# One operand of VectorE's two-input operations moved from SBUF to PSUM in the residual sums, the table scaling and the rotary embedding

## The chip, the core and the metric

One core of one Trainium2 chip runs the whole program; the other cores are idle. The metric is the device time of one execution in microseconds (us). The kernel before took 1189.33 us, the median of three runs that lie between 1189.12 and 1189.84 us.

The engines are named as in the profile: PE is TensorE's matmul, PEld its weight load, DVE is VectorE, ACT is ScalarE, POOL is GpSimd and SP is SyncE, which issues the weight DMAs. SBUF is the working memory. PSUM is the memory that matmuls write, here eight banks of 128 x 512 f32.

## The reference

The program computes two transformer blocks on 256 tokens of width 1024, in f32. Cut to what the change touches:

```
x = x + conv(norm(x));  x = x + mem_attention(norm(x), mem);  x = x + swiglu(norm(x))
k = rope(norm(x) @ w_k);  q = rope(norm(x) @ w_q)      # only 16 of 64 features of a head turn
x = x + diff_attention(q, k, v);  x = x + mem_attention(...);  x = x + swiglu(...)
x = norm(x, g_final);  h = norm(x, g_pre)              # first block ends, second begins
q, k_c, k_s, k_w, k_sw = rope(h @ w_in ...)            # 64 of 64 features turn, then sparse attention
x = x + norm(attention @ w_out);  x = x + norm(conv_swiglu(norm(x)))
rope: out1 = r1 * cos - r2 * sin,  out2 = r1 * sin + r2 * cos
```

## The kernel before

Activations are kept with features on the partitions: x is 8 chunks of 128 features by 256 tokens, and a pair of chunks fills one PSUM bank. Every projection is computed in three matmuls per weight tile, from a high part and a low part of weights and activations. A weight panel of 128 x 1024 is loaded by SP into one of six stage buffers. ACT then writes its high part `whi` (L276), and DVE or POOL subtracts to get the low part `wlo` (L278), from two operands in SBUF. Both go into a ring of five panels, so that the preparation runs five panels ahead of PE.

`gemm` (L392 on) runs over the panels and accumulates up to four banks (`acc`, six buffers). Its last `tail` panels are done bank by bank, so that the banks close one after another and `evac(b, ps)` of each is issued while PE works on the next. `resid` (L435 on) is the evacuation that ends a sublayer: it adds the bank to x, splits the new x times the next norm's gain into a high and a low part (`to_set`, L431 to L433, into S0 or S1), and adds its square to the norm's sum (`Stats.add`, ACT then POOL). It is used five times: after the convolution, both memory attentions, the first feed forward (with two targets, S0 and S1) and the differential attention. `last` (L947 on) does the same after the second feed forward, where two norms follow one another. The sum of squares is folded (`sfold`, L355), summed over the partitions by small matmuls (L361), raised to -1/2 on POOL, and spread over the partitions by a matmul with the identity into an `aux` bank (`spread`, L375 on), from which ACT copies it to SBUF as `Rb` (L381).

`tables` (L820) and `tables2` (L1000) multiply cosine and sine by that factor. `roped_k` and `roped` (L828 to L845) turn the keys and queries of the differential attention: a shuffle swaps the halves, two products follow and then the sum. The keys' sum is written in two halves of 64 partitions. `rope2` (L1008) does the same in the second block.

The differential attention runs a list of steps (`DIFF_SEQ`): q0 and q1 are projections of two heads' queries, a0, a1, ... the scores and softmax of a head (L867, L868 on PE, then `masked`, L324, on DVE), V0 and V1 the values, b the transposed weights, c the values' sum, f the norm of two heads (L908 to L923). PE runs them in the order written. The second block's attention has a like list (`ATT_SEQ`).

The tile framework places every semaphore. A planner with a cost model of its own orders each engine's queue, so that the order on DVE and ACT need not be the order of the program. Two engines that access one PSUM bank are made to take turns. A pool's tag with `bufs=2` gives two buffers in turn. The tag `sq` is that of the squares in `Stats` and of the window in the second block (L1070).

Of the kernel before, what the change touches and what calls it, by code (L numbers as in the profile page):

```python
# [21 lines left out]
F32 = mybir.dt.float32  # L22
# [14 lines left out]
# ---------------------------------------------------------------- layout of the inputs  # L37
# [23 lines left out]
# order of the steps of the two attention parts that share the tensor engine with their projections:  # L61
# a: scores and softmax of a head, b: weights transposed, c: values, f: norm of two heads; the rest are projections
# [8 lines left out]
def _constants():  # L71
    c = np.zeros((128, NCST), np.float32)

    def put(name, a):
        o, n = COFF[name]
        c[:, o:o + n] = a

    i = np.arange(128)
    put("ident", np.eye(128))
    low = np.where(i[None, :] <= i[:, None], 0.0, NEG)  # L80
    put("mask0D", np.concatenate([np.zeros((128, 128)), low], 1))
    put("pair", np.concatenate([np.eye(30), np.eye(30), np.zeros((68, 30))]))
    put("maskUD", np.concatenate([np.where(i[None, :] > i[:, None], 0.0, NEG), low], 1))
    blk = np.arange(32)
    mc = np.zeros((128, 2, 32))
    for t in range(2):
        ok = (blk[None, :] < 15) & (blk[None, :] * 16 + 31 <= (t * 128 + i)[:, None])
        mc[:, t] = np.where(ok, 0.0, NEG)
    put("maskC", mc.reshape(128, 64))
    put("rowv", np.stack([(i >= 31), np.ones(128)], 1))  # L90
    inv = (np.float32(500000.0) ** (-np.arange(0, 16, 2, dtype=np.float32) / np.float32(16))).astype(np.float32)
    f, sg = np.zeros((128, 1), np.float32), np.zeros((128, 1), np.float32)
    for p in range(128):
        d = p % 64
        if d < 16:
            f[p], sg[p] = inv[d % 8], (-1.0 if d < 8 else 1.0)
    put("freq", f)
    put("sgn", sg)
    inv2 = (np.float32(10000.0) ** (-np.arange(32, dtype=np.float32) / np.float32(32))).astype(np.float32)
    ang = np.arange(S, dtype=np.float32)[None, :] * inv2[:, None]  # L100
    d = np.array([PERM[p % 64] for p in range(128)])
    put("cos2", np.cos(ang.astype(np.float64))[d % 32])
    put("sin2", np.sin(ang.astype(np.float64))[d % 32] * np.where(d < 32, -1.0, 1.0)[:, None])
    return c


def _layout(I):
# [30 lines left out]
    def sub(w, nk, W):  # L138
        # panels of nk row blocks by W columns, a column group's panels together
        K, M = w.shape[0] // 128, w.shape[1]  # L140
        return w.reshape(K // nk, nk, 128, M // W, W).transpose(3, 0, 2, 1, 4).reshape(-1, nk * W)
# [40 lines left out]
# ---------------------------------------------------------------- the program  # L182
@with_exitstack
def program(ctx: ExitStack, tc: tile.TileContext, A, out):
# [20 lines left out]
    # ---- weight panels: loaded and split ahead of use  # L205
    panels = []
# [81 lines left out]
    # ---- constants  # L288
# [6 lines left out]
    def vc(name, i=0):  # L295
        o, _ = VOFF[name]
        return vecs[:, o + i:o + i + 1]
# [24 lines left out]
    # scores with their mask and times -1/8, and with their least value, the bias of the exponent  # L322
# [3 lines left out]
    # ---- pieces  # L326
# [48 lines left out]
    def spread(r):  # L375
        pb = aux()
        for t in range(2):
            PE.matmul(pb[:, t * 128:(t + 1) * 128], r[:, t:t + 1].to_broadcast([128, 128]), ident,
                      start=(t == 0), stop=True, skip_group_check=True)
        Rb = tmp.tile([128, S], F32, name="Rb", tag="Rb")  # L380
        SC.activation(Rb, pb[:, :S], AF.Copy)  # L381
        return Rb
# [52 lines left out]
    def resid(stats, targets, bias=None):  # L435
        def f(j, ps):
            xp = x[:, 2 * j:2 * j + 2]
            if bias:
                for i in range(2):
                    c = 2 * j + i  # L440
                    V.scalar_tensor_tensor(x[:, c], ps[:, i * S:(i + 1) * S], vc(bias, c), x[:, c],
                                           op0=OP.add, op1=OP.add)
            else:
                V.tensor_tensor(xp, b2(ps), xp, op=OP.add)
            for st, gname, g0 in targets:
                for c in (2 * j, 2 * j + 1):
                    stats.low = to_set(st, c, x[:, c], vc(gname, g0 + c))
            stats.add(xp)
        return f

    # ================================================================ conformer convolution
# [28 lines left out]
    # memory operands  # L480
# [92 lines left out]
    # keys and values in two parts  # L573
# [27 lines left out]
    # layer norm  # L601
# [53 lines left out]
    # ================================================================ memory attention  # L655
# [84 lines left out]
    # rotary angles of the first block, reduced to [-pi, pi]  # L740
# [29 lines left out]
    # ================================================================ gated feed forward  # L770
# [37 lines left out]
    # ================================================================ differential attention  # L808
    rot = [(i + 8 if i < 8 else i - 8) if i < 16 else i for i in range(32)]
    with ExitStack() as es:  # L810
# [9 lines left out]
        def tables():  # L820
            rb = spread(st.r)
            G.memset(k[0:64, :, 1], 0.0)
            G.memset(k[64:128, :, 0], 0.0)
            V.tensor_tensor(cR, cosT, rb, op=OP.mult)
            V.tensor_tensor(sR, sinT, rb, op=OP.mult)

        def roped(dst, g=0):
            def f(j, ps):  # L828
                d = dst[:, 2 * (g + j):2 * (g + j) + 2]
                t = P.tile([128, 2, S], F32, name="rt", bufs=2)  # L830
                V.stream_shuffle(t.rearrange("p a t -> p (a t)"), ps, rot)
                V.tensor_tensor(d, b2(ps), two(cR), op=OP.mult)
                V.tensor_tensor(t, t, two(sR), op=OP.mult)
                V.tensor_tensor(d, d, t, op=OP.add)
            return f

        def roped_k(j, ps):
            t = P.tile([128, 2, S], F32, name="rt", bufs=2)
            t2 = b2(o[:, j % 2, 0:2 * S])
            V.stream_shuffle(t.rearrange("p a t -> p (a t)"), ps, rot)  # L840
            V.tensor_tensor(t2, b2(ps), two(cR), op=OP.mult)
            V.tensor_tensor(t, t, two(sR), op=OP.mult)
            for c in range(2):
                pr = slice(64 * c, 64 * c + 64)
                V.tensor_tensor(k[pr, 2 * j:2 * j + 2, c], t2[pr], t[pr], op=OP.add)  # L845
# [13 lines left out]
        def a_(h):  # L859
            # per component: query tile 0 on keys 0, query tile 1 on keys 0 and 1  # L860
# [17 lines left out]
        def b_(h):  # L878
            # p0 - lam * (sum0 / sum1) * p1; the factor 1 / sum0 joins the norm of the head
# [64 lines left out]
    # ================================================================ second block  # L944
    sa, sb = Stats(), Stats()

    def last(j, ps):  # L947
        xp = x[:, 2 * j:2 * j + 2]
        V.tensor_tensor(xp, b2(ps), xp, op=OP.add)
        sa.add(xp)  # L950
        for c in (2 * j, 2 * j + 1):
            V.tensor_scalar(x[:, c], x[:, c], vc("g_final", c), None, op0=OP.mult)
            to_set(S0, c, x[:, c], vc("g_pre", c))
        sb.add(xp)
# [31 lines left out]
    def norms():  # L986
        # r1 of the first block's last norm, r2 of the norm that follows it
# [12 lines left out]
    def tables2():  # L1000
        RB[0] = spread(rr)
        V.tensor_tensor(cR, cs("cos2"), RB[0], op=OP.mult)
        V.tensor_tensor(sR, cs("sin2"), RB[0], op=OP.mult)
# [4 lines left out]
    def rope2(d, ps, n):  # L1008
        t = P.tile([128, 2, S], F32, name="rt", bufs=2)
        V.stream_shuffle(t.rearrange("p a t -> p (a t)")[:, :n * S], ps[:, :n * S], rot2)  # L1010
        tb = lambda a: a[:, None, :].to_broadcast([128, n, S])
        V.tensor_tensor(d, ps[:, :n * S].rearrange("p (a t) -> p a t", a=n), tb(cR), op=OP.mult)
        V.tensor_tensor(t[:, :n], t[:, :n], tb(sR), op=OP.mult)
        V.tensor_tensor(d, d, t[:, :n], op=OP.add)  # L1014

    # gates: sigmoid = 1 / (1 + exp(-z))
# [35 lines left out]
    # blocks of the compressed branch: both heads' windows with (token pair, feature) on partitions  # L1052
# [24 lines left out]
    # x2, tokens on partitions  # L1077
# [16 lines left out]
    # rows 0 to 29 of a product come from the high part of the windows, rows 30 to 59 from the low part  # L1094
# [50 lines left out]
    # ---- sliding window heads  # L1145
# [44 lines left out]
    # ---- heads with three branches: 4 diagonal blocks, 2 full ones, 2 of the compressed keys  # L1190
# [108 lines left out]
    # ---- output projection, post norm, residual: tokens on partitions  # L1299
    def rms(hs):  # L1300
        # hs: [128, 2] mean squares of the two halves of a row, each over the whole row
# [120 lines left out]
```

## Time and profile before

| | |
|---|---|
| three runs | 1189.12, 1189.33, 1189.84 us |
| profiled execution, first to last instruction (its span) | 1183.8 us; the profile gives no other time of it |
| what lies around the span, against the runs' median | 5.5 us |
| PE busy | 1121.6 us, 95% of the span |
| PEld, DVE, ACT, POOL busy | 1061.5, 829.4, 639.5, 427.3 us |
| TensorE's granted clock, mean | 0.978 of full speed |
| HBM traffic | 160 GB/s over the span |

PE's busy time is modelled from pipelined matmuls. A matmul of 256 columns is shown as some 280 ns long, while the next one starts earlier than that. What PE loses is therefore read from its waits and from the granted clock, not from its busy share. [...]

### The profile page before, as it was taken

How to read it: one execution, taken by the hardware profiler on the slowest of the kernel's cores; microseconds unless marked ns; L12 is line 12 of the kernel's file. 1: busy time of each engine (PE TensorE's matmuls, PEld its weight loads, DVE VectorE, ACT ScalarE, POOL GpSimd, SP SyncE). 2: the span in 40 equal slices, each digit the busy share in tenths (PEclk: the TensorE clock that was granted, in tenths of full speed). 3: DMA queues.
4: the chain of work that ended last, by engine and by line, in shares of the span. 5: the costliest groups of instructions: out<-in, count | busy, mean ns of one | idle time of the engine just before them, and what ended most of it. 6: DMA issues, size and time to landing. Idle time of an engine off the chain costs nothing. (4 is left out here: it accounts for less than half of the span.)

```text
span 1183.8 us, 21512 instructions
## 1 busy us (share of the span) xinstructions
PE 1121.6 (95%) x8418; PEld 1061.5 (90%) x8418; DVE 829.4 (70%) x1452; ACT 639.5 (54%) x1114; POOL 427.3 (36%) x278
## 2 busy tenths in 40 slices
PE   7999988999999999597899999999898998999997
PEld 7998878999999999497899999999887677999986
DVE  6899867585766458777775746654978747787844
ACT  6564474555545354374555444543585645675642
POOL 5999845230000016565344544000654210111300
PEclk9999988999999999898999999999999999999999
DMA  7565534345546545342243554563664114454661
GB/s 266 192 240 211 189 114 158 110 152 192 181 150 225 194 143 182 107 158 89 90 142 125 194 199 163 174 226 121 187 193 177 37 54 160 161 191 157 219 199 36
DMA packets 59798, 191.13 MB, mean 161 GB/s; under 512 B 6752, under 2 KB 10080, under 8 KB 59696
## 3 DMA queue, kind: packets, MB, share of 16 engines
q1 hardware_dynamic: 58288, 187.31, 46.6%
q0 software_dynamic: 688, 1.90, 0.6%
q8 instruction: 66, 1.08, 0.4%
q10 hardware_dynamic: 720, 0.53, 0.1%
q14 instruction: 36, 0.29, 0.1%
HBM read 188.15 MB, written 1.05 MB: 160 GB/s over the span
## 5 line engine op out<-in xcount | busy, mean ns | idle before, releaser
L276 ACT ACTIVATE whi<-wf 128x1024 fp32r<-128x1024 f32 (+3 forms) x382 | 370.5, 985 | 324.0 <-PE acc L407 267.4
L278 DVE TENSOR_TENSOR wlo<-wf,whi 128x1024 fp32r<-128x1024 f32 (+3 forms) x251 | 311.5, 1252 | 166.3 <-ACT whi L276 165.5
L278 POOL TENSOR_TENSOR wlo<-wf,whi 128x1024 fp32r<-128x1024 f32 (+1 forms) x131 | 288.6, 2223 | 175.8 <-ACT whi L276 173.7
L407 PE MATMUL acc<-s0h,whi 128*128 128x256 f32 x1192 | 340.0, 286 | 5.4 <-ACT whi L276 5.4
L407 PE MATMUL acc<-s0h,wlo 128*128 128x256 f32 x1192 | 337.8, 284 | 3.1 <-POOL wlo L278 3.1
L407 PE MATMUL acc<-s0l,whi 128*128 128x256 f32 x1192 | 338.1, 284 | 2.7 <-DVE s0l L433 2.7
L407 PEld LDWEIGHTS acc<-s0h,whi 128*128 128x128 f32 x1192 | 228.7, 192 | 6.3 <-ACT whi L276 5.4
L407 PEld LDWEIGHTS acc<-s0h,wlo 128*128 128x128 f32 x1192 | 228.1, 191 | 4.5 <-POOL wlo L278 4.2
L407 PEld LDWEIGHTS acc<-s0l,whi 128*128 128x128 f32 x1192 | 228.4, 192 | 3.4 <-DVE s0l L433 3.1
L407 PE MATMUL acc<-s1l,whi 128*128 128x256 f32 x736 | 206.9, 281 | 2.7 <-DVE s1l L433 2.7
L407 PE MATMUL acc<-s1h,whi 128*128 128x256 f32 x736 | 206.7, 282 | 0.7 <-ACT s1h L645 0.7
L407 PE MATMUL acc<-s1h,wlo 128*128 128x256 f32 x736 | 206.2, 280 | 0.4 <-POOL wlo L278 0.4
L407 PEld LDWEIGHTS acc<-s1l,whi 128*128 128x128 f32 x736 | 138.9, 189 | 3.6 <-DVE s1l L433 3.3
L407 PEld LDWEIGHTS acc<-s1h,whi 128*128 128x128 f32 x736 | 138.8, 189 | 1.5 <-ACT s1h L645 1.4
L407 PEld LDWEIGHTS acc<-s1h,wlo 128*128 128x128 f32 x736 | 138.6, 188 | 0.6 <-POOL wlo L278 0.6
L338 POOL TENSOR_TENSOR sacc<-sq,sacc 128x512 f32<-128x512 f32 x21 | 33.6, 1600 | 291.9 <-ACT sq L337 291.5
L407 PE MATMUL acc<-hh,wlo 128*128 128x256 f32 x352 | 99.6, 283 | 0.0
L407 PE MATMUL acc<-hl,whi 128*128 128x256 f32 x352 | 99.6, 283 | 0.0
L407 PE MATMUL acc<-hh,whi 128*128 128x256 f32 x352 | 99.6, 283 | 0.0
L539 DVE SCALAR_TENSOR_TENSOR aux<-u,vecs,aux 128x256 f32<-128x256 f32 x174 | 68.6, 477 | 1.3 <-ACT aux L537 1.3
L407 PEld LDWEIGHTS acc<-hh,whi 128*128 128x128 f32 x352 | 67.6, 192 | 0.0
L407 PEld LDWEIGHTS acc<-hh,wlo 128*128 128x128 f32 x352 | 67.6, 192 | 0.0
(373 smaller groups left out, 1746.9 us busy)
## 6 DMA issues: line engine op xcount, KB each, us to landing
wf<-in_gu SPq DMA_DIRECT2D x120, 512.0 KB, 4.0
wf<-in_w_down SPq DMA_DIRECT2D x66, 512.0 KB, 4.0
wf<-in_mem_w_k SPq DMA_DIRECT2D x16, 512.0 KB, 4.0
wf<-in_mem_w_v SPq DMA_DIRECT2D x16, 512.0 KB, 3.5
wf<-in_mem_w_q SPq DMA_DIRECT2D x16, 512.0 KB, 3.5
wf<-in_mem_w_o SPq DMA_DIRECT2D x16, 512.0 KB, 3.9
wf<-in_w_pw SPq DMA_DIRECT2D x24, 256.0 KB, 3.0
wf<-in_gv SPq DMA_DIRECT2D x24, 256.0 KB, 2.6
```

The costliest lines, as they stand in the source:

```text
L276: p["ih"] = SC.activation(p["hi"][:, :W], p["f"][:, :W], AF.Copy)
L278: p["il"] = eng.tensor_tensor(p["lo"][:, :W], p["f"][:, :W], p["hi"][:, :W].bitcast(F32), op=OP.subtract)
L338: self.ins = self.eng.tensor_tensor(self.acc, sq, self.acc, op=OP.add)
L407: PE.matmul(o, l, r, start=(ki == 0 and n == 0 and q == 0), stop=(ki == K - 1 and q == 2), skip_group_check=True)
L539: V.scalar_tensor_tensor(cv[:, c] if k == TAPS - 1 else ai, src, w, ai, op0=OP.mult, op1=OP.add)
```

## The change

The operations keep their number or nearly so, but in each sum and product on DVE one operand is read from PSUM, and some results are written back into the bank that they came from. In `resid` the sum stays in the bank, `to_set` and the square read it there, and a new ACT copy brings it to x. In `last` the two gains are multiplied once (`gfp`), the sum stays in the bank as well, and two ACT copies with the final gain replace the two DVE products. The scale of the tables is read from the `aux` bank. The rotary embedding first multiplies by the sine table (whose signs are turned over), then multiplies the bank in place by the cosine table, shuffles the sine product, and adds it to the bank.

```diff
-            f[p], sg[p] = inv[d % 8], (-1.0 if d < 8 else 1.0)
+            f[p], sg[p] = inv[d % 8], (1.0 if d < 8 else -1.0)
...
-    put("sin2", np.sin(ang.astype(np.float64))[d % 32] * np.where(d < 32, -1.0, 1.0)[:, None])
+    put("sin2", np.sin(ang.astype(np.float64))[d % 32] * np.where(d < 32, 1.0, -1.0)[:, None])
...
-    def spread(r):
+    def spread(r, raw=False):
...
+        if raw:
+            return pb[:, :S]
         Rb = tmp.tile([128, S], F32, name="Rb", tag="Rb")
         SC.activation(Rb, pb[:, :S], AF.Copy)
         return Rb
...
     def resid(stats, targets, bias=None):
         def f(j, ps):
             xp = x[:, 2 * j:2 * j + 2]
+            half = [ps[:, i * S:(i + 1) * S] for i in range(2)]
             if bias:
                 for i in range(2):
                     c = 2 * j + i
-                    V.scalar_tensor_tensor(x[:, c], ps[:, i * S:(i + 1) * S], vc(bias, c), x[:, c],
-                                           op0=OP.add, op1=OP.add)
+                    V.scalar_tensor_tensor(half[i], half[i], vc(bias, c), x[:, c], op0=OP.add, op1=OP.add)
             else:
-                V.tensor_tensor(xp, b2(ps), xp, op=OP.add)
+                V.tensor_tensor(b2(ps), b2(ps), xp, op=OP.add)
             for st, gname, g0 in targets:
-                for c in (2 * j, 2 * j + 1):
-                    stats.low = to_set(st, c, x[:, c], vc(gname, g0 + c))
-            stats.add(xp)
+                for i in range(2):
+                    c = 2 * j + i
+                    stats.low = to_set(st, c, half[i], vc(gname, g0 + c))
+            stats.add(b2(ps))
+            SC.activation(xp, b2(ps), AF.Copy)
         return f
...
         def tables():
-            rb = spread(st.r)
+            rb = spread(st.r, raw=True)
...
+        def turned(ps):
+            t = P.tile([128, 2, S], F32, name="rt", bufs=2)
+            z = tmp.tile([128, 2, S], F32, name="rz", tag="sq")
+            V.tensor_tensor(t, b2(ps), two(sR), op=OP.mult)
+            V.tensor_tensor(b2(ps), b2(ps), two(cR), op=OP.mult)
+            V.stream_shuffle(z.rearrange("p a t -> p (a t)"), t.rearrange("p a t -> p (a t)"), rot)
+            return b2(ps), z
+
         def roped(dst, g=0):
             def f(j, ps):
                 d = dst[:, 2 * (g + j):2 * (g + j) + 2]
-                t = P.tile([128, 2, S], F32, name="rt", bufs=2)
-                V.stream_shuffle(t.rearrange("p a t -> p (a t)"), ps, rot)
-                V.tensor_tensor(d, b2(ps), two(cR), op=OP.mult)
-                V.tensor_tensor(t, t, two(sR), op=OP.mult)
-                V.tensor_tensor(d, d, t, op=OP.add)
+                t, z = turned(ps)
+                V.tensor_tensor(d, z, t, op=OP.add)
             return f
 
         def roped_k(j, ps):
-            t = P.tile([128, 2, S], F32, name="rt", bufs=2)
-            t2 = b2(o[:, j % 2, 0:2 * S])
-            V.stream_shuffle(t.rearrange("p a t -> p (a t)"), ps, rot)
-            V.tensor_tensor(t2, b2(ps), two(cR), op=OP.mult)
-            V.tensor_tensor(t, t, two(sR), op=OP.mult)
+            t, z = turned(ps)
             for c in range(2):
                 pr = slice(64 * c, 64 * c + 64)
-                V.tensor_tensor(k[pr, 2 * j:2 * j + 2, c], t2[pr], t[pr], op=OP.add)
+                V.tensor_tensor(k[pr, 2 * j:2 * j + 2, c], t[pr], z[pr], op=OP.add)
...
+    gfp = const.tile([128, 8], F32, name="gfp")
+    V.tensor_tensor(gfp, vecs[:, VOFF["g_final"][0]:VOFF["g_final"][0] + 8], vecs[:, VOFF["g_pre"][0]:VOFF["g_pre"][0] + 8], op=OP.mult)
 
     def last(j, ps):
         xp = x[:, 2 * j:2 * j + 2]
-        V.tensor_tensor(xp, b2(ps), xp, op=OP.add)
-        sa.add(xp)
-        for c in (2 * j, 2 * j + 1):
-            V.tensor_scalar(x[:, c], x[:, c], vc("g_final", c), None, op0=OP.mult)
-            to_set(S0, c, x[:, c], vc("g_pre", c))
+        V.tensor_tensor(b2(ps), b2(ps), xp, op=OP.add)
+        for i in range(2):
+            c = 2 * j + i
+            to_set(S0, c, ps[:, i * S:(i + 1) * S], gfp[:, c:c + 1])
+        sa.add(b2(ps))
+        for i in range(2):
+            c = 2 * j + i
+            SC.activation(x[:, c], ps[:, i * S:(i + 1) * S], AF.Copy, scale=vc("g_final", c))
         sb.add(xp)
...
     def tables2():
-        RB[0] = spread(rr)
-        V.tensor_tensor(cR, cs("cos2"), RB[0], op=OP.mult)
-        V.tensor_tensor(sR, cs("sin2"), RB[0], op=OP.mult)
+        rb = spread(rr, raw=True)
+        V.tensor_tensor(cR, cs("cos2"), rb, op=OP.mult)
+        V.tensor_tensor(sR, cs("sin2"), rb, op=OP.mult)
+        RB[0] = tmp.tile([128, S], F32, name="Rb", tag="Rb")
+        SC.activation(RB[0], rb, AF.Copy)
...
     def rope2(d, ps, n):
         t = P.tile([128, 2, S], F32, name="rt", bufs=2)
-        V.stream_shuffle(t.rearrange("p a t -> p (a t)")[:, :n * S], ps[:, :n * S], rot2)
+        z = tmp.tile([128, 2, S], F32, name="rz", tag="sq")
+        flat = lambda a: a.rearrange("p a t -> p (a t)")[:, :n * S]
         tb = lambda a: a[:, None, :].to_broadcast([128, n, S])
-        V.tensor_tensor(d, ps[:, :n * S].rearrange("p (a t) -> p a t", a=n), tb(cR), op=OP.mult)
-        V.tensor_tensor(t[:, :n], t[:, :n], tb(sR), op=OP.mult)
-        V.tensor_tensor(d, d, t[:, :n], op=OP.add)
+        pn = ps[:, :n * S].rearrange("p (a t) -> p a t", a=n)
+        V.tensor_tensor(t[:, :n], pn, tb(sR), op=OP.mult)
+        V.tensor_tensor(pn, pn, tb(cR), op=OP.mult)
+        V.stream_shuffle(flat(z), flat(t), rot2)
+        V.tensor_tensor(d, pn, z[:, :n], op=OP.add)
```

The rest of the diff takes comments out.

## Rows read from the trace of the kernel before

**Rows 1.** The page, part 1: busy us, share of the span, instructions.
```profile
PE   1121.6 (95%) x8418; PEld 1061.5 (90%) x8418; DVE 829.4 (70%) x1452; ACT 639.5 (54%) x1114; POOL 427.3 (36%) x278
```

**Rows 2.** Waits of PE, whole span: us in total, times, longest us.
```profile
PE acc L867 <- DVE q L834: 12.5, 1, 12.5
...
PE aux L361 <- POOL sfold L355: 4.3, 2, 2.2
...
PE acc L1199 <- ACT sp L1158: 3.5, 1, 3.5
PE acc L407 <- DVE s0l L433: 2.7, 1, 2.7
PE acc L407 <- DVE s1l L433: 2.7, 3, 1.8
```

**Rows 3.** Stretches of 40 and 5 us: busy of five engines, clock, DMA.
```profile
280.00:320.00 40.00, 40.00 (x342) 40.00 (x341) 24.30 (x29) 18.73 (x23) 0.00 (x0) 1.00 0.57 193
...
485.00:490.00 5.00, 1.71 (x6) 1.56 (x7) 4.90 (x11) 0.00 (x0) 0.00 (x0) 0.50 0.19 76
490.00:495.00 5.00, 5.00 (x24) 4.22 (x24) 4.57 (x23) 3.25 (x16) 0.00 (x0) 0.89 0.00 0
190.00:195.00 5.00, 3.76 (x16) 3.65 (x17) 5.00 (x4) 1.14 (x2) 4.45 (x4) 0.57 0.58 221
195.00:200.00 5.00, 5.00 (x35) 5.00 (x34) 3.72 (x5) 2.28 (x3) 0.08 (x1) 0.75 0.57 196
905.00:910.00 5.00, 3.02 (x10) 2.24 (x11) 4.45 (x26) 3.54 (x17) 0.00 (x0) 0.75 0.81 308
```

**Rows 4.** DVE in order of time, keys and first queries: start, us, count.
```profile
459.82 0.74 DVE L840 STREAM_SHUFFLE rt<-acc 128x512 f32<-128x512 f32 x1
...
463.18 0.76 DVE L840 STREAM_SHUFFLE rt<-acc 128x512 f32<-128x512 f32 x1
...
467.76 5.07 DVE L845 TENSOR_TENSOR k<-o,rt 64x512 f32<-64x512 f32 x2
...
485.37 0.73 DVE L831 STREAM_SHUFFLE rt<-acc 128x512 f32<-128x512 f32 x1
...
487.45 0.69 DVE L834 TENSOR_TENSOR q<-q,rt 128x512 f32<-128x512 f32 x1
```

**Rows 5.** POOL in order of time, the same stretch.
```profile
464.22 19.14 POOL L278 TENSOR_TENSOR wlo<-wf,whi 128x1024 fp32r<-128x1024 f32 x7 [4.61 <-ACT whi L276]
```

**Rows 6.** Groups by line and shape, DVE: busy us, mean ns, idle before.
```profile
L433 DVE SCALAR_TENSOR_TENSOR s1l<-x,vecs,s1h 128x256 fp32r<-128x256 f32 x24 | 21.4, 933 | 1.9 <-ACT s1h L432 1.9
...
L539 DVE SCALAR_TENSOR_TENSOR aux<-u,vecs,aux 128x256 f32<-128x256 f32 x174 | 68.6, 477 | 1.3 <-ACT aux L537 1.3
...
L845 DVE TENSOR_TENSOR k<-o,rt 64x512 f32<-64x512 f32 x8 | 12.7, 1592 | 0.1
...
L433 DVE SCALAR_TENSOR_TENSOR s1l<-acc,vecs,s1h 128x256 fp32r<-128x256 f32 x8 | 3.8, 476 | 10.3 <-ACT s1h L432 10.3
...
L841 DVE TENSOR_TENSOR o<-acc,cR 128x512 f32<-128x512 f32 x4 | 2.7, 686 | 0.1
...
L1165 DVE RECIPROCAL dsm<-dsm 128x2 f32<-128x2 f32 x8 | 1.3, 160 | 0.1
```

**Rows 7.** DVE in order of time after the convolution, at 188 us.
```profile
188.61 5.41 DVE L433 SCALAR_TENSOR_TENSOR s0l<-x,vecs,s0h 128x256 fp32r<-128x256 f32 x3
```

**Rows 8.** DVE in order of time in the second block's attention, from 889 us.
```profile
889.85 2.26 DVE L1164 TENSOR_TENSOR dsm<-dsm 128x2 f32<-128x2 f32 x1
...
899.87 2.83 DVE L1014 TENSOR_TENSOR qn<-qn,rt 128x512 f32<-128x512 f32 x1
```

**Rows 9.** ACT in order of time where both engines read one bank.
```profile
1006.01 0.56 ACT L1369 ACTIVATE t<-acc,vecs 128x256 f32<-128x256 f32 x1 [1.84 <-PE acc L407]
1007.64 0.56 ACT L1369 ACTIVATE t<-acc,vecs 128x256 f32<-128x256 f32 x1 [1.07 <-DVE t L1371]
```

**Rows 10.** Groups by line and shape, ACT: copy of a bank.
```profile
L592 ACT ACTIVATE memK<-acc 128x512 f32<-128x512 f32 x4 | 2.3, 590 | 0.1
```

## The prediction

> **What bounds the kernel now.** I read the busy times first [rows 1]: PE is busy for 1121.6 of 1183.8 us and every other engine far less, so an edit on DVE or ACT pays only where PE waits or where its clock falls. The next view is therefore the list of PE's waits [rows 2]. One wait towers over it: the first scores of the differential attention (L867) wait 12.5 us for the turned queries q (L834). Behind it stand waits for the folded squares (4.3 us in two), for a softmax (3.5), and for the low parts that `to_set` writes (2.7 and 2.7, L433). [...]
>
> Why q is late stands in DVE's order of time [rows 4]. The first pair of keys needs 459.82 to 463.18, 3.36 us. From then on POOL runs seven `wlo` subtractions without a break until 483.36 [rows 5], and DVE's operations with two SBUF operands stretch: two sums of the keys take 5.07 us. The groups say the same [rows 6]: L845, two operands in SBUF, 1592 ns on the mean; L841, one of them in PSUM, 686 ns in the same stretch; L433 933 ns from x but 476 ns from a bank. So an operation with two SBUF operands waits for POOL, and one with a PSUM operand does not.
>
> **Part 1, tables and rotary embedding of the first block.** Per pair of keys there are five operations before and after; what changes is that each of the four products and sums has one operand in PSUM, so I give a pair the undisturbed 3.3 us of the first one. A bank closes every 18 matmuls. A matmul starts every 40/342 = 0.117 us [rows 3], so that is 2.1 us. PE's wait ended with q at 487.45 + 0.69 = 488.14 and began 12.5 us before, at 475.7; q0 and q1 are 96 matmuls, 11.2 us, so the last keys' bank closed at 464.5 and the first at 458.2. DVE is then the slower of the two: four pairs end at 458.2 + 4 x 3.3 = 471.4. The first queries take 485.37 to 488.14 = 2.8 us [rows 4] and end at 474.2, 1.5 us before PE needs them. The wait of 12.5 us goes. What is late next is q1's turn, needed only for a2, behind V0's 48 longer matmuls. PE's half-speed work after the wait, 488.1 to about 491.1 (1.9 us at 0.50, then 0.11/0.5 x 5 = 1.1 us), is 3.0 us long and gives back 1.5. Together 14.0 at most. I take 13, because the planner may set another DVE operation between; the lower end is 4 (the second rival). Below nothing it cannot go through the pairs alone, since no operation is added to them. The cover matters: without the 1.5 us of margin every further microsecond on DVE is one on PE.
>
> Two prices are not in the trace as such. A product written back into its bank: the nearest row is L539, a two-operand operation of half the size that writes PSUM, 477 ns, against 476 for L433 that writes SBUF [rows 6]; no difference taken, 0.1 us a pair at most either way. The shuffle reads SBUF in place of PSUM: with one SBUF source the nearest row is L1165 (tiny), eight times 160 ns on the mean, while beside it the tiny two-operand L1164 once took 2.26 us [rows 6, 8]. I take 0.75 as now [rows 4]; the other end is a wait for the rest of a POOL subtraction, 19.14/7 = 2.7 us at most [rows 5].
>
> **Part 2, the residual sums.** The 56 `to_set` subtractions of the changed sublayers go from x to the bank. Two waits of PE are for them. After the convolution three of these took 5.41 us in the way of POOL [rows 7]; at 0.48 they take 1.4. PE's wait of 2.7 shrinks, but ACT must take turns (below). The low clock behind it is 4.3 us (0.43/0.5 x 5) and 2.5 us long, of which PE works some 5.7: 2.9 us lost. Ends 0 and 5.6; I take 3. After the differential attention 2.7 us in three waits, at full clock; ends 0 and 2.7; I take 2.
>
> On the other side, the bank now keeps two engines taking turns. The trace shows the price: ACT's second half of a bank could start at 1006.57 and started at 1007.64, after DVE's reading [rows 9], a hold of 1.07 us. So a pair's chain is the sum 0.69, two times (ACT 0.48, DVE 0.48, two hand-overs of 0.03), then the copy 0.59 [rows 10] and the square taken alike: about 3.9 us, and 6.0 with two targets, against a bank every 24 x 0.117 = 2.8 us. Chains of different banks may overlap. The next stage's last chunks come 1 us later than they would without turns, and the folded squares 1 to 2.4 us. Queued behind a waiting `to_set` are, on ACT, the next `whi`, and on DVE the next `wlo`; five panels in the ring, some 14 us of PE's work, cover them. A first fold waited for 2.2 us already [rows 2] and is put on POOL later. I take a loss of 2; ends 0 and 8 (six stage ends at 1.3). The added copies are 20 of 0.59 us and 8 halves of some 0.48, 15.6 us on ACT, which was busy for 54% [rows 1]; hidden, else part of the 8.
>
> **Part 3, the end of the first block and the second block's rope.** In `last` eight DVE products leave and DVE's subtractions no longer wait; the fold's second wait (2.1 of the 4.3) lies behind them, and the chain to `tables2` saves one ACT copy. Ends -1 and 5; I take 2.5. In the attention a sum of `rope2` took 2.83 in place of 0.68, just ahead of the softmax for which PE waited 3.5 us, and the clock was at 0.75 over 5 us afterwards [rows 2, 3, 8]: 2.5 us low, about 1.2 lost. Ends 0 and 4.7; I take 2.5. `rz` shares the tag `sq` with the second window: that window must wait for q's second turn. The window is needed for its branch only several microseconds later; nothing taken, else 2 us.
>
> **The sum.** 13 + 3 + 2 - 2 + 2.5 + 2.5 = 21 us. The profiled span of 1183.8 becomes 1162.8, and with the 5.5 us around it 1168.3 against the median of 1189.33.
>
> [...] An operation with one operand in PSUM is not slower here than one with both in SBUF that is left alone: L841 took 686 ns, and L834 0.69 us once POOL was idle [rows 4 to 6]. [...]
>
> **Rivals.**
> *The wait moves one step on* (chance 0.15). The part of the attention after a0 keeps its two-operand sums in SBUF (norm of two heads), now with POOL's subtractions closer behind one another because 12 us of slack are gone. For: DVE still had tiny operations held 2.26 us by POOL [rows 8]. Against: POOL needs 2.7 us a panel and PE as much. Price two more holds of 2.3 us and a low clock of 1.5 to 2.5 us: 1168.3 + 6.7 = 1175.
> *The shuffle waits for POOL* (0.12). Its SBUF source is new. Five shuffles on the path wait some 1.9 us, as each of the two sums did that took 5.07 [rows 4]: the pairs end at 471.4 + 7.6 = 479.0 and the first queries at 483.7, so PE waits 8.0 us and stays at low clock; part 1 gives 4 to 5, `rope2` nothing. Of the 21, 8.5 and 2.5 go: 1179. Against it stands L1165. [...]
> *The turns starve the next stage* (0.07, slower). On ACT a `to_set` waits for DVE's subtraction, that one stands behind a `wlo`, and this one waits for the `whi` that is queued behind the `to_set`'s successors. If eight subtractions of a stage end each wait out a 1.2 us `wlo`, that is 10 us more, and the 14 us cover of the ring is gone when the chain's own 4 us are added. Price for a stage end 5 us of wait and 2.5 of low clock; four of the six stage ends cost 30 us, over the 23 gained elsewhere: 1189 + 7 = 1196. It decides from the fourth stage end on. For: L433 stood in such a queue [rows 7]. Against: the planner knows these waits.
> *No change* (0.04). Two-operand operations wait for another reason, say their SBUF output. Against: L841 writes SBUF in 686 ns, undisturbed. 1189.
>
> **Chances and range.** The forecast has 0.62, with 1160 to 1175 as its own range. The first two rivals lie at 1175 and 1179, with spread to 1182; the low end adds the better ends of parts 2 and 3, 11 us: 1157. So 1157 to 1182 leaves out the last two rivals (0.11) and a little below. A measurement tells from no change what differs by over 0.2%, 2.4 us: faster 0.88, within 0.05, slower 0.07.
>
> **What would show it.** L867's wait under 2 us and the clock at 1.00 from 475 to 495; L845's successor at 0.7 us; the shuffle at 0.75 (else the second rival); L433 near 476 everywhere; ACT's idle before `to_set` ended by DVE's L433 with about 0.5 us each; PE's waits for `sfold` no longer than 5.5 us in all. It is wrong if L867 still waits over 5 us, or if PE waits for `whi` or `wlo` at the stage ends.

## The result and the profile after

The changed kernel takes 1176.83 us (median of four runs, 1176.31 to 1182.42) against 1189.59 us for the kernel before in the same series (1189.12 to 1192.37): a ratio of 0.9899, 95% interval 0.9878 to 0.9919. That is 12.8 us faster. The forecast was 1168.3 us, so the time lies inside the range of 1157 to 1182 and 8.5 us above the forecast, just outside the 1160 to 1175 that the forecast had as its own range. A second series of runs gave 1176.49 us and 0.9874 (0.9851 to 0.9897).

The busy times of the changed kernel, as in [rows 1]:

```profile
PE 1121.0 (95%) x8418; PEld 1061.5 (90%) x8418; DVE 787.4 (67%) x1445; ACT 650.7 (55%) x1141; POOL 425.3 (36%) x278
```

DVE has 42 us less work and ACT 11 more, while PE is as busy as before. What changed is where PE waits, as in [rows 2]:

```profile
PE aux L361 <- POOL sfold L355: 10.5, 7, 2.9
...
PE acc L1116 <- POOL win L1090: 3.4, 1, 3.4
PE acc L1214 <- ACT sp L1173: 2.9, 1, 2.9
PE aux L712 <- DVE p L708: 2.3, 1, 2.3
...
PE acc L409 <- DVE s0l L435: 1.6, 1, 1.6
...
PE acc L409 <- DVE s1l L435: 0.3, 1, 0.3
```

The wait of 12.5 us for q is gone from the list. Those for the low parts fell from 5.4 to 1.9 us. In exchange the folded squares cost 10.5 us in place of 4.3, a wait for the window `win` is new, and a wait for a softmax of the second memory attention (`p`, L712) grew from 0.5 to 2.3 us. DVE's order of time shows the keys, as in [rows 4]:

```profile
459.57 0.69 DVE L834 TENSOR_TENSOR rt<-acc,sR 128x512 f32<-128x512 f32 x1 [1.90 <-PE acc L409]
460.17 0.69 DVE L835 TENSOR_TENSOR acc<-acc,cR 128x512 f32<-128x512 f32 x1
...
460.78 0.74 DVE L836 STREAM_SHUFFLE rz<-rt 128x512 f32<-128x512 f32 x1
461.55 1.39 DVE L850 TENSOR_TENSOR k<-acc,rz 64x512 f32<-64x512 f32 x2
...
468.77 1.38 DVE L850 TENSOR_TENSOR k<-acc,rz 64x512 f32<-64x512 f32 x2
...
475.10 0.69 DVE L843 TENSOR_TENSOR q<-rz,acc 128x512 f32<-128x512 f32 x1
```

Two sums of the keys take 1.38 us at 468.77, where two took 5.07 at 467.76 before. POOL is as full at that point as it was, yet its seven subtractions, as in [rows 5], now take 16.58 us in place of 19.14:

```profile
465.54 16.58 POOL L278 TENSOR_TENSOR wlo<-wf,whi 128x1024 fp32r<-128x1024 f32 x7 [7.60 <-ACT whi L276]
```

The groups of DVE by line and shape, as in [rows 6]:

```profile
L435 DVE SCALAR_TENSOR_TENSOR s1l<-acc,vecs,s1h 128x256 fp32r<-128x256 f32 x32 | 14.8, 476 | 13.5 <-ACT s1h L434 13.2
...
L836 DVE STREAM_SHUFFLE rz<-rt 128x512 f32<-128x512 f32 x8 | 5.9, 741 | 0.1
L835 DVE TENSOR_TENSOR acc<-acc,cR 128x512 f32<-128x512 f32 x8 | 5.5, 692 | 0.0
...
L850 DVE TENSOR_TENSOR k<-acc,rz 64x512 f32<-64x512 f32 x8 | 5.5, 687 | 0.1
```

The subtractions of `to_set` take 476 ns instead of 933, the keys' sums 687 instead of 1592, and the shuffle from SBUF 741.

The two traces can be laid side by side, since PE issues the same projections in both. Each matmul of a projection is paired with the same one of the other trace. By how much its start moves from one stretch to the next is:

| stretch (us of the trace before) | change, us |
|---|---|
| start, code untouched (to 162) | -1.1 |
| convolution's residual (to 196) | -2.1 |
| memory attention, feed forward (to 453) | -1.2 |
| norm ahead of the keys (453 to 459) | **+5.7** |
| keys, queries to the first scores (to 492) | **-14.2** |
| differential attention, its residual (to 587) | -3.6 |
| second memory attention, its residual (to 658) | +3.2 |
| second feed forward (to 840) | -1.0 |
| `last` and the two norms (to 855) | +2.5 |
| rows of x2 (to 864) | -1.5 |
| compressed branch's windows (864 to 887) | **+5.9** |
| to the end | -1.8 |

The sum is -9.2, the difference of the spans (1174.5 against 1183.8) -9.3. In a second trace of the changed kernel the three bold rows are +5.3, -14.2 and +4.9; other rows differ from these by up to some 3 us, so a small row alone settles nothing.

Both large losses are read on POOL, in order of time. Ahead of the keys (the last square on ACT, before and after, then POOL after):

```profile
447.30 0.62 ACT L337 ACTIVATE sq<-x 128x512 f32<-128x512 f32 x1
```

```profile
449.37 0.58 ACT L337 ACTIVATE sq<-acc 128x512 f32<-128x512 f32 x1
```

```profile
447.27 1.85 POOL L338 TENSOR_TENSOR sacc<-sq,sacc 128x512 f32<-128x512 f32 x1 [4.36 <-ACT sq L337]
449.54 2.39 POOL L278 TENSOR_TENSOR wlo<-wf,whi 128x1024 fp32r<-128x1024 f32 x1 [0.42 <-ACT whi L276]
451.88 1.27 POOL L338 TENSOR_TENSOR sacc<-sq,sacc 128x512 f32<-128x512 f32 x1
453.24 0.72 POOL L355 TENSOR_TENSOR sfold<-sacc 128x256 f32<-128x256 f32 x1
```

ACT began the last square at 449.37, where it had begun it at 447.30 before, although PE was by then some 4.3 us ahead of the trace before. It ended at 449.95, when POOL had just taken a weight subtraction, so the fold ended at 453.96 and PE waited 2.9 us for it. The clock fell to 0.66 over the next stretch; in windows of 1 us it was 0.50 from 456 to 458, with 6 and 7 matmuls, and 1.00 from 459 on, with 11 (windows of the changed kernel, columns as in [rows 3]):

```profile
475.00:480.00 5.00, 5.00 (x37) 4.71 (x36) 3.69 (x10) 2.60 (x3) 5.00 (x4) 1.00 0.71 249
...
455.00:460.00 5.00, 4.54 (x27) 4.35 (x26) 1.19 (x3) 0.00 (x0) 2.93 (x2) 0.66 0.22 52
870.00:875.00 5.00, 1.96 (x9) 1.96 (x10) 0.92 (x2) 1.49 (x3) 3.91 (x6) 0.67 0.60 203
```

At 475 us, where the long wait began, PE now runs at full clock. At 870 us, with the clock at 0.67, stands the second loss. POOL there, in order of time, before and after:

```profile
861.14 3.40 POOL L1073 TENSOR_TENSOR winf<-kc,vecs 128x240 f32<-128x240 f32 x4 [0.84 <-DMA kc<-kcv]
```

```profile
866.36 2.48 POOL L278 TENSOR_TENSOR wlo<-wf,whi 128x1024 fp32r<-128x1024 f32 x1 [7.09 <-ACT whi L276]
868.80 2.37 POOL L1088 TENSOR_TENSOR winf<-kc,vecs 128x240 f32<-128x240 f32 x2
871.88 1.11 POOL L1090 TENSOR_TENSOR win<-winf,win 128x480 fp32r<-128x480 f32 x1 [0.72 <-ACT win L1089]
```

POOL idles 7.09 us, runs a subtraction and then begins the first window at 868.80; before, it did so at 861.14.

### The profile page after: what moved, and what is told of

The parts are those of the page before. It is cut to its first block, busy times and chain, and to the rows that moved or that the text cites. A ratio compares the mean times of both kernels' runs of the same rounds, so it can differ in the third digit from the quotient of the medians.

```text
span 1174.5 us, 21545 instructions
## 1 busy us (share of the span) xinstructions
PE 1121.0 (95%) x8418; PEld 1061.5 (90%) x8418; DVE 787.4 (67%) x1445; ACT 650.7 (55%) x1141; POOL 425.3 (36%) x278
## 4 chain that ended last, share of the span: by engine, by line
PE 44%; DVE 2%; issue 2%; POOL 1%; ACT 1%; POOLq 0%; DVEq 0%; ACTq 0%
PE acc L409 38%; PE acc L1116 1%; PE acc L1214 1%; DVE wlo L278 1%; POOL sacc L338 1%; PE acc L723 0%; PE acc L1275 0%; PE acc L1279 0%; PE aux L1256 0%; PE acc L1368 0%; POOL sfold L355 0%; PE acc L1276 0%; PE acc L1211 0%; PE acc L692 0%; POOL rmr L1320 0%
## 5 line engine op out<-in xcount | busy, mean ns | idle before, releaser
L278 DVE TENSOR_TENSOR wlo<-wf,whi 128x1024 fp32r<-128x1024 f32 (+3 forms) x251 | 319.0, 1280 | 180.5 <-ACT whi L276 179.6
L278 POOL TENSOR_TENSOR wlo<-wf,whi 128x1024 fp32r<-128x1024 f32 (+1 forms) x131 | 285.3, 2194 | 183.5 <-ACT whi L276 183.3
L409 PEld LDWEIGHTS acc<-hl,whi 128*128 128x128 f32 x352 | 67.6, 192 | 0.0
```

The source lines that it names most:

```text
L278: p["il"] = eng.tensor_tensor(p["lo"][:, :W], p["f"][:, :W], p["hi"][:, :W].bitcast(F32), op=OP.subtract)
L409: PE.matmul(o, l, r, start=(ki == 0 and n == 0 and q == 0), stop=(ki == K - 1 and q == 2), skip_group_check=True)
```

## The experiments

Theory 1 has three parts: (a) a DVE operation with both operands in SBUF waits for POOL's running subtraction, and the rope of the keys gained by losing that; (b) sums kept in the bank make the square wait behind the parts that `to_set` cuts from the same bank, and the late squares cost about what the faster subtractions gain; (c) `rz` holds the buffers of tag `sq` that the window needs. The rivals: the sums carry part of the gain; the new order of operations, not the operand, gained; POOL's queue, not the buffer, holds the window. The first four experiments ran on one chip and the others on another; each series has its own runs of the kernel before, with medians of 1191.27 and 1191.69 us, and every ratio is against those.

**Rope alone.** `resid` and `last` are those of the kernel before; rope and tables are changed:

```diff
-                V.tensor_tensor(b2(ps), b2(ps), xp, op=OP.add)
+                V.tensor_tensor(xp, b2(ps), xp, op=OP.add)
...
-            stats.add(b2(ps))
-            SC.activation(xp, b2(ps), AF.Copy)
+            stats.add(xp)
```

> Only the rotary part of the change (products into the bank, shuffle last, tables from the bank); the residual sums and `last` go through x in SBUF as before. Theory 1 (the whole gain comes from the rope of the keys, which no longer waits for POOL, and the sums kept in the bank lose about as much at the next stage's start as they gain): L867's wait of 12.5 us is gone, the wait for `sfold` ahead of the keys is gone again, the wait for the window `win` (some 3.4 us) is still there, and the time is near 1173 us, 16 less than before and 3 to 4 less than the whole change. Rival (the sums carry part of the gain, their late squares are chance): 1180 us or more, some 3 us above the whole change. A second rival (the gain in the keys needs the sums to end early): L867 still waits over 5 us.

Measured: 1177.65 us, ratio 0.9875 (0.9860 to 0.9889). Its waits of PE:

```profile
PE aux L361 <- POOL sfold L355: 4.8, 2, 2.5
...
PE acc L1108 <- POOL win L1082: 3.4, 1, 3.4
```

The wait for q is gone, the one for `sfold` ahead of the keys too, and the wait for `win` is there. The waits came as theory 1 said. The time came out 4 to 5 us above its figure, at that of the whole change. The rope alone carries the whole gain. Against the trace before, this one loses 3.0 us at `last` and the two norms, although `last` is that of the kernel before. So a loss in that stretch need not come from late squares; what else makes it no run shows.

**Sums alone.** The other half: `resid` and `last` changed, rope and tables as before.

```diff
-            t, z = turned(ps)
...
+            V.stream_shuffle(t.rearrange("p a t -> p (a t)"), ps, rot)
+            V.tensor_tensor(t2, b2(ps), two(cR), op=OP.mult)
+            V.tensor_tensor(t, t, two(sR), op=OP.mult)
```

> Only the sums kept in the bank (residual sums and `last`); the rope and its tables as before. Theory 1: the gains after the convolution, the differential attention and `last` (2.1 + 1.2 + 2.7 + 2.4 us in the two traces) and the losses to late folded squares (5.7 ahead of the keys, 3.5 and 2.9 later) nearly cancel, a little to the bad: L867 waits some 12 us as before, PE waits for `sfold` some 10 us in all, no wait for `win` (nothing shares its buffer), time 1189 to 1194 us. Rival (the sums carry part of the gain): under 1184 us. Rival (the start of the keys is late anyway, so the loss ahead of them is hidden in the 12.5 us wait): that wait shrinks to some 7 us and the time is near 1185.

Measured: 1191.78 us, ratio 1.0004 (0.9992 to 1.0016): no change. Its waits of PE:

```profile
PE acc L871 <- DVE q L838: 11.5, 1, 11.5
PE aux L361 <- POOL sfold L355: 10.4, 6, 2.9
```

As theory 1 has it, the late squares are there and so is the wait for q, only 1.0 us shorter: the loss ahead of the keys is not hidden in it. The sums as the change writes them bring nothing.

**The window's buffer.** The changed kernel with

```diff
-            wf = tmp.tile([128, 2, S], F32, name="winf", tag="sq")
+            wf = tmp.tile([128, 2, S], F32, name="winf", tag="sacc")
```

> The changed kernel, with the window's tile `winf` on the tag `sacc` (free after the norms) instead of `sq`, which it shares with the shuffled half `rz`. Theory (the first window is split late because its buffer is held by an `rz` that a turn of the rope still needs): PE's wait L1116 <- POOL win (3.4 us) goes, the first window's sums on POOL run near 861 us instead of 868.8, the clock stays at 1.00 from 870 to 880, and the time is 1171 us, some 5 to 6 less than the changed kernel. Rival (POOL's queue of weight subtractions, reordered by the faster work ahead, holds the window): the wait stays over 2 us and the time within 1.5 us of the changed kernel's.

Measured: 1175.12 us, ratio 0.9861 (0.9846 to 0.9876). POOL's order of time:

```profile
852.03 2.11 POOL L1088 TENSOR_TENSOR winf<-kc,vecs 128x240 f32<-128x240 f32 x3 [0.53 <-DMA kc<-kcv]
```

The window is begun at 852 us, released by its own DMA, and PE's wait for `win` has left the list. The shared tag is the cause: the rival would have kept the wait. How the tag acts is not as theory 1c has it, though. The tag's two buffers are used in turn, so the first window takes the one of the `rz` of the first `qw`, whose last reader in the changed kernel is this sum:

```profile
849.48 0.69 DVE L1029 TENSOR_TENSOR qw<-acc,rz 128x512 f32<-128x512 f32 x1
```

From 850.17 on that buffer was free, and the window's data had landed by 851.91, yet the first window was begun at 868.80. In between POOL ran three subtractions, and twice it sat idle until ACT had the `whi` of the next one, the second time for 7.09 us: the window stood behind them in POOL's queue. So the tag moved the window's place in that queue; why the planner put it there no run shows.

The time is another matter: 1175.12 is 4 us above the expected 1171 and 1.4 us below the 1176.49 of the changed kernel, and the two intervals overlap. Side by side with the second trace of the changed kernel, PE gains 5.4 us between 866 and 881 us and loses small amounts elsewhere. By this run alone the price stays open; the run with both edits below settles it.

**The square first.** The changed kernel; in `resid` (and likewise in `last`)

```diff
+            stats.add(b2(ps))
             for st, gname, g0 in targets:
...
-            stats.add(b2(ps))
             SC.activation(xp, b2(ps), AF.Copy)
```

> The changed kernel, with the square of a summed bank put ahead of the low and high parts that `to_set` makes of it (in the residual sums and in `last`), nothing else. Theory (ACT and DVE take turns on a bank, so the square that comes last is about 2 us later than before, POOL starts a weight subtraction of 2.4 us ahead of it, and the folded squares for which PE waits are late): PE's waits for `sfold` fall from 10.5 us to under 5, the clock ahead of the keys stays at 1.00, and the time is near 1168 us. Rival (the parts now come later by the square's 0.6 us, and PE waits for the low parts at the stage starts instead): waits for L435 grow from 1.9 us to 5 or more and the time is 1175 to 1180.

Measured: 1167.51 us, ratio 0.9800 (0.9780 to 0.9819). POOL ahead of the keys, then PE's waits:

```profile
441.75 1.35 POOL L338 TENSOR_TENSOR sacc<-sq,sacc 128x512 f32<-128x512 f32 x1
443.18 0.74 POOL L355 TENSOR_TENSOR sfold<-sacc 128x256 f32<-128x256 f32 x1
449.13 0.70 POOL L372 TENSOR_TENSOR rr<-ms,mhalf 128x2 f32<-128x2 f32 x1 [5.22 <-DVE ms L370]
```

```profile
PE aux L361 <- POOL sfold L355: 4.4, 2, 3.2
...
PE acc L409 <- DVE s0l L435: 0.6, 1, 0.6
PE acc L409 <- DVE s1l L435: 0.6, 1, 0.6
```

The fold is done at 443.92 instead of 453.96, ten microseconds earlier, and PE's waits for the parts did not grow. The late squares cost 9.0 us against the 1176.49 of the other series, 8.8 by the ratios. With the same rope, the sums in the bank are now worth 10 us over the rope alone.

**Both edits.** The square first and the window on `sacc`, nothing else.

> The changed kernel with both edits: the square ahead of the parts, and the window's tile on the tag `sacc`. If the late squares and the window's buffer are two separate causes, their gains add: 1167.5 from the square alone less about 5 (3.4 us of wait and half of the 6.8 us of low clock behind it) is 1162 us, with neither the wait for `win` nor one for `sfold` ahead of the keys. Rival (the softmax behind the window, for which PE waits 2.3 to 3.4 us, takes over what the window gives back): 1165 us or more.

Measured: 1161.50 us, ratio 0.9749 (0.9726 to 0.9772), the fastest version here: 30 us below the kernel before and 15 below the change. Neither `win` nor `sfold` ahead of the keys is waited for; one fold is left, that of `last`:

```profile
PE acc L1214 <- ACT sp L1173: 3.4, 1, 3.4
PE aux L361 <- POOL sfold L355: 3.2, 1, 3.2
```

The gains add: 6.0 us below the square alone (in the other series) are the window's. The softmax behind it grew from 2.3 to 3.4 us of wait, so it takes back about one.

**One operand back in SBUF.** The changed kernel; the cosine product goes to SBUF, all else in its new order:

```diff
-            V.tensor_tensor(b2(ps), b2(ps), two(cR), op=OP.mult)
+            V.tensor_tensor(dst, b2(ps), two(cR), op=OP.mult)
```

> The changed kernel, but in the first block's rope the cosine product goes to SBUF (where it went before) instead of its bank; the order of the five operations and the shuffle from SBUF stay. So the last sum alone has two SBUF operands again. Theory A (a DVE operation with both operands in SBUF waits out POOL's running subtraction): the sums of the keys L850 take 1.5 us or more on the mean instead of 0.69, all others stay at 0.69 to 0.75, PE waits 5 to 9 us for q ahead of the first scores, and the time is 6 to 10 us above the changed kernel's 1177. Rival B (the new order of the five operations brought the gain, or the bank that is written back): L850 stays near 0.7 us, no wait for q, and the time is within 2 us of the changed kernel's.

Measured: 1185.73 us, ratio 0.9956 (0.9930 to 0.9982), 9.2 us above the changed kernel in the same series. PE waits, then the groups of DVE and the order of time on DVE and on POOL:

```profile
PE acc L872 <- DVE q L843: 6.0, 1, 6.0
```

```profile
L850 DVE TENSOR_TENSOR k<-o,rz 64x512 f32<-64x512 f32 x8 | 12.8, 1600 | 0.1
...
L836 DVE STREAM_SHUFFLE rz<-rt 128x512 f32<-128x512 f32 x8 | 5.8, 731 | 0.0
```

```profile
463.30 1.39 DVE L850 TENSOR_TENSOR k<-o,rz 64x512 f32<-64x512 f32 x2
...
467.15 3.50 DVE L850 TENSOR_TENSOR k<-o,rz 64x512 f32<-64x512 f32 x2
```

```profile
467.29 19.56 POOL L278 TENSOR_TENSOR wlo<-wf,whi 128x1024 fp32r<-128x1024 f32 x7 [7.38 <-ACT whi L276]
```

Only the keys' sums are slow, and only from the moment POOL starts: two take 1.39 us at 463.30 and 3.50 at 467.15. The product, which reads the bank, and the shuffle, which reads one operand from SBUF, keep their 0.7 us beside it. Rival B is out.

**POOL emptied instead.** The kernel before with the low parts of two weights on DVE:

```diff
-          dn0="v", K="v", q="g", V="g", o="g", mq1="gvv", mo1="vgv", gu1="gv", gv1="v",
+          dn0="v", K="v", q="v", V="v", o="g", mq1="gvv", mo1="vgv", gu1="gv", gv1="v",
```

> The kernel before, unchanged in its rope and its sums, with the low parts of the panels of w_q and w_vs computed on DVE instead of POOL, so that POOL runs no subtraction while the keys are turned. Theory A (POOL is what holds the two-operand operations): L842 and L845 take 0.7 us each throughout instead of 1.6 on the mean; seven subtractions of some 1.2 us are new on DVE, so the queries still come late, PE waiting 5 to 9 us at L867 instead of 12.5. Rival (they are slow by their SBUF output or by something else on DVE): L845 stays above 1.3 us and the wait grows to 15 us or more.

Measured: 1183.89 us in a single run, 7.8 below the median before and 2.5 below the fastest of its ten runs. The group of the keys' sums and PE's wait:

```profile
L845 DVE TENSOR_TENSOR k<-o,rt 64x512 f32<-64x512 f32 x8 | 5.4, 680 | 0.1
```

```profile
PE acc L867 <- DVE q L834: 4.0, 1, 4.0
```

With the rope of before and an idle POOL (it runs nothing from 456.4 to 500 us) the sums take 680 ns, as quick as from a bank, although DVE now carries the subtractions too. That is theory 1a from the other side. The wait fell further than I had expected.

**The change once more**, as a yardstick.

> The changed kernel itself once more, on the same chip as the others, as their yardstick: 1177 us, 0.990 of the kernel before. If its time here differs by over 2 us from that, the differences between runs of different calls are to be read with that much doubt.

Measured: 1176.49 us, 0.9874 (0.9851 to 0.9897), within 0.4 us of the first time.

## Why the prediction was right, and what it mis-sized

- **The bound and part 1 held.** Taken 13, measured 14.2 between the norm and the first scores. Its signs came: no wait at L867's successor and clock 1.00 at 475 us; L850 at 687 ns. One sign of part 2 did not come: I had named 5.5 us as the most that PE would wait for `sfold`, and it waited 10.5. The two prices that no row showed came out as taken: the product written into its bank 692 ns, the shuffle from SBUF 741.
- **The gains of part 2 held.** 2.1 after the convolution (taken 3), 2.7 after the differential attention (taken 2), of the 3.6 there.
- **The turns on a bank were mis-sized.** I took a loss of 2, with 8 as the other end. The two stretches that lost to late folds cost 8.2 (5.7 ahead of the keys, 2.5 at `last`); in the trace with the square first they lose nothing (0.0 and -0.6 against the trace before), and its time is 9 us lower. That all of the 2.5 at `last` is the squares' is not settled, since the rope alone loses 3.0 there. I had computed the chain as if its links ran back to back, 3.9 to 6.0 us. They don't: ahead of the keys, where each bank has two targets, the parts of the last two banks run from 440.70 to 448.50 on ACT and DVE in turn, with `whi` and `wlo` between. The square stands behind them in the program; as soon as it shares their bank it inherits their delay. Before, it read x and ran at 447.30 ahead of the last low parts (447.96 to 449.87). I also wrote that the first fold is put on POOL later, and did not price what runs on POOL ahead of it, a subtraction of 2.4 us.
- **A term was missing: the second memory attention.** It lost 3.2 us, and 3.3 still with the square first, so this is not the turns on a bank. PE's wait for the softmax `p` grew by 1.8 us there; the last section shows why. The rope alone does not have this loss (-0.4), the sums alone have it (+3.4).
- **`rz` on `sq` was the second mis-sized term.** I took nothing, "else 2 us"; the pair of traces shows 5.9 and the run with both edits 6.0. I had looked at the second window and its buffer; it was the first one that lost its place in POOL's queue, and the clock fell to 0.67 behind a wait of 3.4 us.
- **Part 3 gave less than taken.** For `last` and the chain behind it I took a gain of 2.5; `last` lost 2.5 and the rows of x2 gave back 1.5. Of the 2.5 taken for the second block's rope 1.4 came, with the wait behind q's turn down from 3.5 to 2.9 us; in the second trace of the changed kernel that wait is 3.4 and 0.8 came.
- **The base was off.** I put 5.5 us around the span. Here a profiled run of 1176.31 us has a span of 1174.5; in every profiled run of this study 1.7 to 1.8 us lie around it. So the profiled execution before took some 1185.6 us (an estimate from that), 3.7 below its median. The traces differ by 9.3 us and the medians by 12.8 for that reason.
- **Sum.** I took 23 us of gains and 2 of losses. In the table the rows that gain add to 26.5 and the rows that lose to 17.3: 9.2 instead of 21. That the median came out 12.8 and not 9.3 better is the fast profiled run before, and that the time lies inside the range is in part luck: the range went up to 1182 for the sake of the first two rivals, and neither of them came.
- **The rivals.** The shuffle does not wait for POOL. The wait did not move to the attention behind a0. The turns did not starve a stage by the ring of panels, as that rival had it (PE's wait for `whi` is the 5.4 us of the start); they cost through the squares. "No change" fell with the two runs on the operand and on POOL.
- **The operand in a bank.** That it is not slower held within 7 ns: with POOL emptied, the rope of before takes 680 ns for a sum from SBUF; the changed one takes 687 with one operand in a bank. In the run with one operand put back, beside a busy POOL, a sum with two SBUF operands took 1600 ns on the mean and a shuffle with one SBUF operand 731.

## What to carry to other kernels

A DVE operation with both operands in SBUF was worth moving here, where POOL worked beside it and PE waited behind it: the keys' sums went from 1592 to 687 ns and PE's wait of 12.5 us went. What moves forward by it must be followed too: the softmax of the second memory attention met a POOL subtraction that it had missed before, and PE's wait for it grew from 0.5 to 2.3 us. When a value stays in a bank, put the reader that feeds the longest chain (here the square that starts the norm) first, because the bank's readers on two engines took turns here (ACT idled 1.50 us until DVE's `s0l` was done and began the square at 190.94), and the fold was done at 443.92 with the square named first and at 453.96 with it named last. Before borrowing a tag, list every tile that uses it later, and ask of each when PE needs it.

## What I had not expected of the hardware

POOL is slowed as well. Its seven subtractions took 19.14 us beside DVE's two-operand sums [rows 5], 19.56 in the run with one operand put back and 16.58 beside the changed rope: 2.7 to 2.8 us each against 2.4. And an operation left with two SBUF operands holds up those behind it: after the convolution `wlo` on DVE took 2.78 us where it takes 1.21 undisturbed. The subtractions of `to_set` behind it are fast now (0.86 for two), yet PE still waits 1.6 us for them, which is the 1.57 that `wlo` lost (no run tests this):

```profile
184.41 2.78 DVE L278 TENSOR_TENSOR wlo<-wf,whi 128x1024 fp32r<-128x1024 f32 x1 [0.20 <-ACT whi L276]
187.12 0.86 DVE L435 SCALAR_TENSOR_TENSOR s0l<-acc,vecs,s0h 128x256 fp32r<-128x256 f32 x2
...
191.22 1.21 DVE L278 TENSOR_TENSOR wlo<-wf,whi 128x1024 fp32r<-128x1024 f32 x1
```

Nor is it two SBUF operands alone that POOL holds up. The softmax of the second memory attention scales `p`, one SBUF tensor, by a column of factors. Two such products took 0.62 us in the trace before, where POOL's next subtraction began at 603.73; in the changed kernel they start 0.37 us behind one and take until it is over:

```profile
602.95 0.62 DVE L704 TENSOR_SCALAR p<-p,sm 128x256 f32<-128x256 f32 x2
```

```profile
587.89 2.40 DVE L708 TENSOR_SCALAR p<-p,sm 128x256 f32<-128x256 f32 x2
```

```profile
587.52 2.35 POOL L278 TENSOR_TENSOR wlo<-wf,whi 128x1024 fp32r<-128x1024 f32 x1
```

PE's wait for `p` grew by the same 1.8 us. With the rope alone PE waits 0.5 us for `p`, as before; in every run with the sums in the bank 2.2 to 2.6. The shuffle, with one SBUF operand as well, was not held: at 467.55 us, while POOL ran its subtractions, it took 0.75.
